# Seven block products in eleven groups instead of seven, with the corner sums taken in mid-group

## The chip, the cores and the metric

The kernel runs on one core of one Trainium2 chip. The metric is the device time of one execution in microseconds (us). TensorE (PE) multiplies matrices into PSUM, which has eight banks here: four for accumulators (`acc_ps`), four for small results (`sm_ps`). VectorE (DVE) and ScalarE (ACT) do elementwise work, GpSimd (POOL) a little of it, and SyncE (SP) starts the loads. Each engine runs its own instructions strictly in the order in which the program has them, and waits where an operand or a buffer isn't ready.

## The reference

A trunk of two layers over 256 tokens of width 2048: an mLSTM mixer, a gated ConvFFN, a differential attention, a second ConvFFN, all in float32. What touches the change:

```python
def mlstm_mixer(xn, w_in, b_igate, b_fgate, w_hnorm, w_out):
    proj = xn @ w_in
    q, k, v, o, ig, fg = jnp.split(proj, M_SPLITS, axis=-1)
    ...
    h = rms_norm(h.transpose(0, 2, 1, 3), w_hnorm).astype(xn.dtype)
    h = h.reshape(B, S, M_HV) * jax.nn.sigmoid(o)
    return h @ w_out

def shared_kv(h, g_kv, w_kv, pos):
    kv = rms_norm(h, g_kv) @ w_kv
    k, v = jnp.split(kv, (A_HQK,), axis=-1)
    ...

def diff_attention(xn, k, v, pos, w_q, lam_q1, lam_k1, lam_q2, lam_k2, g_subln, w_o, lambda_init):
    ...
    lam = (jnp.exp(jnp.sum(lam_q1 * lam_k1)) - jnp.exp(jnp.sum(lam_q2 * lam_k2)) + lambda_init)
    ...
        pd = p[:, :, 0] - lam * p[:, :, 1]
        outs.append(jnp.einsum('bhqk,bkhv->bqhv', pd.astype(vb.dtype), vb))
    ...
    return o.reshape(B, S, A_HV) @ w_o
```

Heads are 256 wide in V; `o` is the output gate. Each of the four projections that the change speaks of (gate `o`, `w_out`, attention's V, `w_o`) is a product of 256 x 2048 by 2048 x 2048.

## The kernel before, in words

**Products in split form.** TensorE multiplies float32 operands in a reduced form, so each operand is split in a high and a low part: ACT copies the high part of a weight tile (`w2`, L376), DVE subtracts it from the tile for the low part (L377). A product is three matmuls: high by high, low by high, high by low.

**Groups.** A projection by tokens (`gemm_tokens`, L437) runs over four groups of 512 columns. A group takes 16 k-tiles of 128 rows; two accumulators `a` and `b` of 128x512, one for each half of the tokens, collect it. Four k-tiles come with one load of 1 MB (`raw`, four buffers), and are split in two granules of two k-tiles, each into one `w2` buffer. There are five `w2` buffers (`HL`), so a split waits until the granule five earlier has been multiplied. A dense granule is 12 matmuls of 128x512.

**Sevenths.** `gemm_sevenths` does four of the 16 k-tiles of a group, the quad, by Winograd's form of the 2x2 block product: for each pair of k-tiles seven block products of 128x256 instead of eight, times three, 42 matmuls in all (L493) instead of 24 of 128x512. It needs differences of the weights (`diff`, DVE, L449 to L451), splits of the three blocks and the four differences (L458, L459), and mixed forms of the other operand (`mix`: four sums on DVE, L531 to L534, a split on ACT and DVE, L536 and L537). Two more accumulators `c` and `d` (named `mix`) collect what belongs to more than one corner. They are buffers of `sm_ps`. At the group's end the corners are summed. In the gate projection `mixed_up` does it: a copy on ACT (L559), four sums of 128x256 on DVE (L560 to L563), two of 128x512 into a and b (L564, L565). In the output projections `mixed_in` sums straight into the residual stream, a copy and seven instructions (L572 to L579).

**Where.** `OUT_AT = (8, 10)` sets the k-tiles of the pairs, that is the third load of a group. Sevenths are used in the gate projection for groups 1 and 2, in `m_w_out` for groups 1 to 3, in `w_o` for groups 2 and 3. Gate groups 0 and 3, `m_w_out` group 0, `w_o` groups 0 and 1 and all of attention's V are dense. The FFN's down projections have sevenths of their own, with other k-tiles. The mixed forms of the norm's output (`x_mixed`) are made at once ahead of the gate projection by `mix_again`; those of the heads' outputs come with the head whose tiles they are, `mix_scaled` in `turned` and `placed`.

**What sets the order.** `tick()` counts granules, and `later(n, fn)` emits a step n granules on: head steps, parameters, lambda (`lambda_col`, a small matmul into `lam_ps`, L916, nine granules after the parameters' loads). The order of each engine is then fixed at build by a scheduler from priorities (program order) and readiness, so a later step can stand ahead of an earlier one. `evac_o` (gate), `evac_v` and `residual` empty the accumulators at a group's end: in the gate projection tanh on ACT (L804) and a product on DVE (L805), then transposes on TensorE (`hn_ps`, L357), split into `mo` (L306, L307), which are the operands of `m_w_out`.

Of the kernel before, what the change touches and what calls it, by code (L numbers as in the profile page):

```python
# [10 lines left out]
F32 = mybir.dt.float32  # L11
# [27 lines left out]
RAW = 4  # L39
OUT_AT = (8, 10)  # L40
MIXED = (4, 12, 20)
# [27 lines left out]
def trunk(  # L69
# [25 lines left out]
    def small_ps(name):  # L95
        return sm_ps.tile([P, 512], F32, tag="sm", name=name)
# [366 lines left out]

    def gemm_sevenths(xs, mixed, w, col0, groups, evac, at):


        kn, raws = len(xs), {}
        for g in groups:
# [3 lines left out]
            while k0 < kn:  # L472
                if k0 in at:
                    if c is None:
                        c, d = small_ps("mix"), small_ps("mix")
                    parts = sevenths(w, col0 + g * G, k0, min(2, (kn - k0) // 2))
                    for p, (b1, b2, b3, t1, t3, t2, t4) in enumerate(parts):
# [16 lines left out]
                        if p < len(parts) - 1:  # L494
                            tick()
                    k0 += 4
                else:
# [7 lines left out]
                tick()  # L505
            evac(g, (a, b), (c, d))

# [45 lines left out]

    def mixed_up(ps, mix):

        (a, b), (c, d) = ps, mix
        u = tmp("mx")
        x, y = block(F32, "mixed_a"), block(F32, "mixed_b")
        act.activation(x[1], c[:, :T], AF.Copy)  # L559
        dve.tensor_tensor(u, c[:, T:], x[1], op=ALU.add)  # L560
        dve.tensor_tensor(y[1], d[:, T:], u, op=ALU.add)
        dve.tensor_tensor(x[0], d[:, :T], u, op=ALU.add)
        dve.tensor_tensor(y[0], d[:, :T], y[1], op=ALU.add)  # L563
        dve.tensor_tensor(a, a, x[2], op=ALU.add)  # L564
        dve.tensor_tensor(b, b, y[2], op=ALU.add)  # L565

# [97 lines left out]
    def mlstm(norm):  # L664
# [85 lines left out]

        def evac_v(g, ps):
            for c in range(2):
                h = 2 * g + c
                v[h] = [scaled_split(ps[t][:, c * VD:(c + 1) * VD], norm.rt[:, t:t + 1], f"mv{h}_{t}", T + 2) for t in range(2)]
                for vh, vl, _ in v[h]:
                    pool.memset(vh[:, T:].bitcast(F32), 1.0)
                    pool.memset(vl[:, T:].bitcast(F32), 0.0)
                later(1 + 4 * c, lambda h=h: weights(h))
# [37 lines left out]

        def evac_o(g, ps, mix=None):
            if mix is not None:
                mixed_up(ps, mix)
            for c in range(2):  # L800
# [26 lines left out]
        later_parameters_in()  # L827
        x_mixed = {k: mix_again(xs[k], xs[k + 1]) for k in OUT_AT}
        gemm_tokens(xs, w, 2 * HQK + HV, [0], evac_o)
        gemm_sevenths(xs, x_mixed, w, 2 * HQK + HV, [1, 2], evac_o, OUT_AT[:1])  # L830
        gemm_tokens(xs, w, 2 * HQK + HV, [3], evac_o)
        return outs, outs_mixed

# [90 lines left out]
    def attention(norm):  # L924
# [54 lines left out]

        def evac_v(g, ps):  # L980
            for c in range(2):
# [30 lines left out]
        gemm(norm.sets[1], w_kv, 0, range(8), rotated(k, "ak", softmax))  # L1012
        gemm_tokens(norm.sets[1], w_kv, AQK, range(4), evac_v)
        return outs, outs_mixed
# [3 lines left out]
    def later_parameters_in():  # L1018

        with tc.issue_after(loads[-1].ins):  # L1020
# [5 lines left out]
            later_layers.append(rotary_tables())  # L1026
        later(9, lambda: later_layers.append(lambda_col()))

# [9 lines left out]
    norm_f0 = Norm([(gains, G_F0)], "f0")  # L1038
    gemm_tokens(outs, m_w_out[0], 0, [0], residual(norm_f0))
    gemm_sevenths(outs, outs_mixed, m_w_out[0], 0, range(1, NG - 1), residual(norm_f0), OUT_AT[:1])  # L1040
    gemm_sevenths(outs, outs_mixed, m_w_out[0], 0, [NG - 1], residual(norm_f0), OUT_AT[:1])

# [4 lines left out]
    gemm_tokens(outs, w_o[0], 0, range(2), residual(norm_f1), lead=2)  # L1047
    gemm_sevenths(outs, outs_mixed, w_o[0], 0, range(2, NG), residual(norm_f1), OUT_AT[:1])

# [91 lines left out]
```

## Time and profile before

| what | us |
|---|---|
| median of 3 runs (2253.45 to 2253.83) | 2253.77 |
| the profiled execution | 2253.21 |
| its span | 2251.4 |
| TensorE busy | 2239.6 |
| DVE busy | 1789.7 |
| ACT busy | 1292.0 |

The profiled execution is 1.8 us longer than its span, which is what lies around the first and last instruction. A busy TensorE is a chain of pipelined matmuls; its share of the span says how little it waits. A row of the view of groups ends with busy time, mean ns of one, and idle time before it with the releasers. In a timeline the first two figures are start and duration in us, and the bracket names what an engine waited for.

By the timeline, the stages that matter lie at: gate projection 233 to 305, `m_w_out` 305 to 396, attention's V 1318 to 1420, `w_o` 1420 to 1515.

### The profile page before, as it was taken

To read this page: it belongs to the slowest core of one execution; us is meant where nothing else is said; L and a number is where in the kernel's file an instruction comes from. 1 tells how busy PE (TensorE), PEld (TensorE's weight loads), DVE (VectorE), ACT (ScalarE), POOL (GpSimd) and SP (SyncE) were. 2 spreads that over 40 slices of the span, in tenths; PEclk is the share of its full clock that TensorE was granted. 3 is DMA by queue.
4 is the path that set the end of the run, shared out by engine and by line. 5 is a ranking of instruction groups with operands and counts; after the bars stand their busy time and mean duration, and the time that the engine had idled before them with its cause. 6 is when DMAs were issued, how large, how long until landed. Compare 5 with 4: busy or idle time off the path is not lost.

```text
span 2251.4 us, 33430 instructions
## 1 busy us (share of the span) xinstructions
PE 2239.6 (99%) x12843; PEld 1954.1 (87%) x12843; DVE 1789.7 (79%) x2964; ACT 1292.0 (57%) x1994; POOL 125.0 (6%) x305
## 2 busy tenths in 40 slices
PE   9999999999999999999999999999999999999998
PEld 9888888888888888888888888888888888888888
DVE  5756778887888877879998885677877988778896
ACT  5456655655555555656654556566555555556554
POOL 0014200000000000000022103200000000000000
PEclk9999999999999999999999999999999999999999
DMA  7554546555555755545566555465555457555464
GB/s 265 188 169 157 166 171 205 192 191 187 187 170 179 242 187 187 187 150 203 189 208 194 163 167 169 150 206 187 187 187 187 156 191 239 191 189 191 146 215 150
DMA packets 325348, 419.04 MB, mean 186 GB/s; under 512 B 9070, under 2 KB 238788, under 8 KB 325188
## 3 DMA queue, kind: packets, MB, share of 16 engines
q1 hardware_dynamic: 325156, 416.89, 56.4%
q8 instruction: 101, 1.65, 0.3%
q14 instruction: 59, 0.48, 0.1%
q10 hardware_dynamic: 32, 0.01, 0.0%
HBM read 414.77 MB, written 2.10 MB: 185 GB/s over the span
## 4 chain that ended last, share of the span: by engine, by line
PE 97%; DVE 1%; POOL 1%; issue 1%; ACT 0%; DMA 0%; DVEq 0%; SPq 0%; POOLq 0%
PE acc L411 54%; PE acc L503 16%; PE acc L437 12%; PE mix L493 6%; PE acc L493 4%; PE acc L634 2%; PE acc L521 1%; PE val_ps L335 1%; PE turn_ps L231 1%; PE as_ps L955 0%; DVE w L377 0%; POOL rs_u L279 0%; POOL rs_u L280 0%; DMA pos_i<-in_positions_dram 0%; POOL rs_u L281 0%
## 5 line engine op out<-in xcount | busy, mean ns | idle before, releaser
L377 DVE TENSOR_TENSOR w<-raw,w 128x1024 fp32r<-128x1024 f32 x679 | 825.9, 1220 | 280.1 <-ACT w L376 277.5
L376 ACT ACTIVATE w<-raw 128x1024 fp32r<-128x1024 f32 x679 | 713.9, 1058 | 491.7 <-PE acc L411 324.8
L411 PE MATMUL acc<-x_f,w 128*128 128x512 f32 (+1 forms) x5632 | 988.1, 337 | 0.0
L411 PEld LDWEIGHTS acc<-x_f,w 128*128 128x128 f32 x5632 | 861.7, 188 | 123.2
L503 PE MATMUL acc<-w,hid 128*128 128x512 f32 x1080 | 268.2, 394 | 0.0
L503 PEld LDWEIGHTS acc<-w,hid 128*128 128x128 f32 x1080 | 195.4, 188 | 39.0
L411 PE MATMUL acc<-x_at,w 128*128 128x512 f32 (+1 forms) x1024 | 182.1, 338 | 0.0
L411 PEld LDWEIGHTS acc<-x_at,w 128*128 128x128 f32 x1024 | 156.8, 188 | 22.2 <-issue 0.3
L458 ACT ACTIVATE w<-diff 128x1024 fp32r<-128x1024 f32 x89 | 94.1, 1057 | 111.1 <-DVE diff L451 81.7
L417 ACT ACTIVATE low<-acc 128x256 f32<-128x256 f32 x216 | 79.3, 386 | 135.4 <-PE acc L411 132.6
L459 DVE TENSOR_TENSOR w<-diff,w 128x1024 fp32r<-128x1024 f32 x89 | 108.7, 1221 | 40.9 <-ACT w L458 40.3
L437 PE MATMUL acc<-w,x_a 128*128 128x512 f32 x576 | 138.0, 396 | 0.0
L437 PEld LDWEIGHTS acc<-w,x_a 128*128 128x128 f32 x576 | 106.8, 188 | 24.2
L493 PE MATMUL mix<-w,mix 128*128 128x256 f32 x801 | 119.3, 281 | 0.0
L418 DVE TENSOR_TENSOR acc<-acc,low 128x256 f32<-128x256 f32 x216 | 84.5, 430 | 37.7 <-ACT low L417 37.3
L493 PEld LDWEIGHTS mix<-w,mix 128*128 128x128 f32 x801 | 107.0, 188 | 2.4 <-DVE w L459 0.2
L848 ACT ACTIVATE c<-u,conv 128x256 f32<-128x256 f32 x176 | 98.2, 593 | 5.5 <-DVE u L846 5.2
L939 POOL TENSOR_TENSOR sw<-sw,sin_t 32x256 f32<-32x256 f32 x32 | 42.0, 1328 | 1033.8 <-DVE sw L938 1022.5
L458 ACT ACTIVATE w<-raw 128x768 fp32r<-128x768 f32 x89 | 74.7, 840 | 37.9 <-PE acc L503 27.4
L437 PE MATMUL acc<-w,x_at 128*128 128x512 f32 x384 | 91.8, 396 | 0.0
L459 DVE TENSOR_TENSOR w<-raw,w 128x768 fp32r<-128x768 f32 x89 | 84.6, 951 | 2.8 <-ACT w L458 2.7
L493 PE MATMUL acc<-w,hid 128*128 128x256 f32 x450 | 86.3, 281 | 0.0
(302 smaller groups left out, 2320.4 us busy)
## 6 DMA issues: line engine op xcount, KB each, us to landing
raw<-in_w_up_dram SPq DMA_DIRECT2D x176, 1024.0 KB
raw<-in_w_down_dram SPq DMA_DIRECT2D x79, 1024.0 KB
raw<-in_m_w_in_dram SPq DMA_DIRECT2D x46, 1024.0 KB
raw<-in_w_kv_dram SPq DMA_DIRECT2D x32, 1024.0 KB
raw<-in_m_w_out_dram SPq DMA_DIRECT2D x16, 1024.0 KB
raw<-in_w_q_dram SPq DMA_DIRECT2D x16, 1024.0 KB
raw<-in_w_o_dram SPq DMA_DIRECT2D x16, 1024.0 KB
raw<-in_w_down_dram SPq DMA_DIRECT2D x15, 512.0 KB
```

The lines of the kernel that those rows point to most:

```text
L376: act.activation(w2[:, :hc, 0], part, AF.Copy)
L377: dve.tensor_tensor(w2[:, :hc, 1], part, w2[:, :hc, 0].bitcast(F32), op=ALU.subtract)
L411: pe.matmul(to, a, b, start=(k == 0 and o == 0), stop=(k == kn - 1 and o == len(ops) - 1))
L417: act.activation(low, p[:, T:], AF.Copy)
L418: dve.tensor_tensor(p[:, :T], p[:, :T], low, op=ALU.add)
L437: pe.matmul(ps[t], a[:, s], b, start=(k == 0 and o == 0), stop=(k == kn - 1 and o == 2))
L458: act.activation(w2[:, :m, 0], src, AF.Copy)
L459: dve.tensor_tensor(w2[:, :m, 1], src, w2[:, :m, 0].bitcast(F32), op=ALU.subtract)
L493: pe.matmul(to, u, v, start=start and o == 0, stop=end and o == 2 and to is not a and to is not b, skip_group_check=True)
L503: pe.matmul(ps, u[:, s], v, start=(k0 + i == 0 and o == 0), stop=(k0 + i == kn - 1 and o == 2), skip_group_check=True)
L634: pe.matmul(ps[j], a, b, start=(k == 0 and o == 0 and j % 2 == 0), stop=(k == KD - 1 and o == 2), skip_group_check=True)
L848: act.activation(c, u, AF.Identity, bias=cw[:, 3, f:f + 1], scale=cw[:, 2, f:f + 1])
```

## The change

- `OUT_AT` becomes (4, 6): the quad is a group's second load, and the heads whose outputs get mixed forms are 2 and 3 instead of 4 and 5.
- `gemm_sevenths` takes `mid`. With it, c and d are buffers of `acc_ps`, and `mid` is emitted right behind the quad's last granule; the evacuation gets what it returns. `mixed_up` is cut in two: `mixed_sums` (copy and four sums) for mid-group, `mixed_up` (two sums into a and b) for the end. For the output projections `mid` is `mixed_in`.
- The mixed forms of the norm's output are made by `forms_of`, two and four granules into the projection's first group, for the gate and for attention's V.
- Sevenths in attention's V for groups 1 to 3, and in `m_w_out` for group 0 too: 11 groups (gate 2, `m_w_out` 4, V 3, `w_o` 2) instead of 7 (2, 3, 0, 2).
- Lambda comes 40 granules after the parameters instead of 9.

```diff
-OUT_AT = (8, 10)
+OUT_AT = (4, 6)
...
-    def gemm_sevenths(xs, mixed, w, col0, groups, evac, at):
+    def gemm_sevenths(xs, mixed, w, col0, groups, evac, at, mid=None):
...
                     if c is None:
-                        c, d = small_ps("mix"), small_ps("mix")
+                        if mid is None:
+                            c, d = small_ps("mix"), small_ps("mix")
+                        else:
+                            c, d = (acc_ps.tile([P, 2 * T], F32, tag="acc", name="mix") for _ in range(2))
...
+                    if mid is not None and k0 == at[-1]:
+                        sums = mid(g, (c, d))
                     k0 += 4
...
-            evac(g, (a, b), (c, d))
+            evac(g, (a, b), (c, d) if mid is None else sums)
...
-    def mixed_up(ps, mix):
-
-        (a, b), (c, d) = ps, mix
+    def forms_of(xs, forms):
+        for n, k in enumerate(OUT_AT):
+            later(2 + 2 * n, lambda k=k: forms.update({k: mix_again(xs[k], xs[k + 1])}))
+
+    def mixed_sums(g, mix):
+
+        c, d = mix
...
         dve.tensor_tensor(y[0], d[:, :T], y[1], op=ALU.add)
-        dve.tensor_tensor(a, a, x[2], op=ALU.add)
-        dve.tensor_tensor(b, b, y[2], op=ALU.add)
+        return x[2], y[2]
+
+    def mixed_up(ps, sums):
+        for p, x in zip(ps, sums or ()):
+            dve.tensor_tensor(p, p, x, op=ALU.add)
...
-        def evac_v(g, ps):
+        def evac_v(g, ps, sums=None):
+            mixed_up(ps, sums)
...
-        x_mixed = {k: mix_again(xs[k], xs[k + 1]) for k in OUT_AT}
-        gemm_tokens(xs, w, 2 * HQK + HV, [0], evac_o)
-        gemm_sevenths(xs, x_mixed, w, 2 * HQK + HV, [1, 2], evac_o, OUT_AT[:1])
-        gemm_tokens(xs, w, 2 * HQK + HV, [3], evac_o)
+        col, x_mixed = 2 * HQK + HV, {}
+        forms_of(xs, x_mixed)
+        gemm_tokens(xs, w, col, [0], evac_o)
+        gemm_sevenths(xs, x_mixed, w, col, [1, 2], evac_o, OUT_AT[:1], mixed_sums)
+        gemm_tokens(xs, w, col, [3], evac_o)
...
-        gemm_tokens(norm.sets[1], w_kv, AQK, range(4), evac_v)
+        xs, x_mixed = norm.sets[1], {}
+        forms_of(xs, x_mixed)
+        gemm_tokens(xs, w_kv, AQK, [0], evac_v)
+        gemm_sevenths(xs, x_mixed, w_kv, AQK, range(1, 4), evac_v, OUT_AT[:1], mixed_sums)
...
-        later(9, lambda: later_layers.append(lambda_col()))
+        later(40, lambda: later_layers.append(lambda_col()))
...
-    gemm_tokens(outs, m_w_out[0], 0, [0], residual(norm_f0))
-    gemm_sevenths(outs, outs_mixed, m_w_out[0], 0, range(1, NG - 1), residual(norm_f0), OUT_AT[:1])
-    gemm_sevenths(outs, outs_mixed, m_w_out[0], 0, [NG - 1], residual(norm_f0), OUT_AT[:1])
+    gemm_sevenths(outs, outs_mixed, m_w_out[0], 0, range(NG), residual(norm_f0), OUT_AT[:1], mixed_in)
...
-    gemm_sevenths(outs, outs_mixed, w_o[0], 0, range(2, NG), residual(norm_f1), OUT_AT[:1])
+    gemm_sevenths(outs, outs_mixed, w_o[0], 0, range(2, NG), residual(norm_f1), OUT_AT[:1], mixed_in)
```

Three places show how the order moves. The line numbers of the changed kernel are its own: L509 is a dense matmul of `gemm_sevenths`, L497 a block product, L569 the copy and L570 to L573 the sums of `mixed_sums`, L578 `mixed_up`, L817 the gate's tanh. The bracket at a row's end names the engines or load queues (DMAHW) that the instruction waits for.

First TensorE at the end of gate group 1. Before, group 1's products into d (`mix_2658`) stand last, and group 2 opens a and b (`acc_2773`, `acc_2774`) at once:

```order
L493 MATMUL mix_2658<-w2_2674,mix_2283 128x256
L493 MATMUL mix_2658<-w2_2674,mix_2284 128x256
L493 MATMUL mix_2658<-w2_2674,mix_2283 128x256 x2
L493 MATMUL mix_2658<-w2_2674,mix_2284 128x256
L493 MATMUL mix_2658<-w2_2674,mix_2283 128x256
L503 MATMUL acc_2773<-w2_2777,x_a_0_172 128x512 [waits Activation_49]
L503 MATMUL acc_2773<-w2_2777,x_a_0_172 128x512
L503 MATMUL acc_2774<-w2_2777,x_a_0_172 128x512 x2
```

Now dense granules stand last, and group 2's a (`acc_2763`) runs ahead of its b, with a wait for DVE at its first matmul:

```order
L509 MATMUL acc_2581<-w2_2734,x_a_15_635 128x512 x3
L509 MATMUL acc_2582<-w2_2734,x_a_15_635 128x512 x3
L509 MATMUL acc_2763<-w2_2767,x_a_0_172 128x512 [waits DVE_49]
L509 MATMUL acc_2763<-w2_2767,x_a_0_172 128x512 x2
L509 MATMUL acc_2763<-w2_2767,x_a_1_175 128x512 x3
L509 MATMUL acc_2763<-w2_2830,x_a_2_244 128x512 x3
L509 MATMUL acc_2763<-w2_2830,x_a_3_247 128x512 x3
L497 MATMUL acc_2763<-w2_2853,x_a_5_291 128x256 x3
```

In the built program `acc_2763` has the bank of `mix_2615`, group 1's c, and the wait is for L570, its last reader.

Second ACT at the same place. Before, the copy of c stands ahead of the splits of group 2's quad:

```order
L376 ACTIVATE w2_2846<-raw_2829 128x2x512 [waits PE_49]
L306 ACTIVATE mo3_2578<-hn_ps_2570,half_h_145 128x256 [waits DVE_49]
L559 ACTIVATE mixed_a_2752<-mix_2657 128x256
L458 ACTIVATE w2_2869<-raw_2863 128x3x256 [waits DMAHW6_49,PE_49,Activation_49]
L458 ACTIVATE w2_2872<-diff_2865 128x4x256 [waits DVE_49,PE_49,Activation_49]
```

Now it stands behind the third of these splits, whose buffer held `w2_2734`:

```order
L458 ACTIVATE w2_2856<-diff_2849 128x4x256 [waits DVE_49,Activation_49]
L306 ACTIVATE mo1_2567<-hn_ps_2559,half_h_145 128x256 [waits DVE_49]
L306 ACTIVATE mo2_2575<-hn_ps_2570,half_h_145 128x256 [waits PE_49]
L458 ACTIVATE w2_2859<-raw_2847 128x3x256 [waits PE_49,Activation_49]
L306 ACTIVATE mo3_2578<-hn_ps_2570,half_h_145 128x256 [waits DVE_49]
L569 ACTIVATE mixed_a_2678<-mix_2615 128x256
```

The copy has moved from ahead of a split for the next group to behind one that waits for TensorE.

Third DVE at the end of gate group 2. Before, the first sum (L560) stands behind head 3's last `mo` and ahead of group 3's next split:

```order
L377 TENSOR_TENSOR w2_3061<-raw_3059,w2_3061 128x2x512 [waits DMAHW1_49,DVE_49,Activation_49]
L377 TENSOR_TENSOR w2_3076<-raw_3059,w2_3076 128x2x512 [waits DVE_49,Activation_49]
L307 SCALAR_TENSOR_TENSOR mo7_2811<-hn_ps_2803,half_h_145,mo7_2811 128x256 [waits Activation_49]
L560 TENSOR_TENSOR mx_2955<-mix_2861,mixed_a_2956 128x256 [waits Activation_49]
L377 TENSOR_TENSOR w2_3093<-raw_3091,w2_3093 128x2x512 [waits DMAHW2_49,DVE_49,Activation_49]
```

Now a split that group 3 needs (`w2_3083`, in the buffer of group 2's last weights) and head 3's mixed forms (`sum_2821`, `mix_2827`) stand ahead of it:

```order
L307 SCALAR_TENSOR_TENSOR mo7_2814<-hn_ps_2806,half_h_145,mo7_2814 128x256 [waits Activation_49]
L377 TENSOR_TENSOR w2_3083<-raw_3081,w2_3083 128x2x512 [waits DMAHW2_49,Activation_49]
L539 TENSOR_TENSOR sum_2821<-mx_2817 128x128 [waits Activation_49]
L537 TENSOR_TENSOR sum_2821<-mx_2817,mx_2818 128x128 [waits Activation_49]
L538 TENSOR_TENSOR sum_2821<-sum_2821,mx_2817 128x128 [waits DVE_49]
L540 TENSOR_TENSOR sum_2821<-mx_2818,sum_2821 128x128 [waits DVE_49]
L543 TENSOR_TENSOR mix_2827<-sum_2821,mix_2826 128x512 [waits Activation_49]
L570 TENSOR_TENSOR mx_2907<-mix_2845,mixed_a_2908 128x256 [waits Activation_49]
```

Group 3's first matmul waits for this L570 in the same way: its a has the bank of `mix_2845`, group 2's c.

More of the change, by code (lines that the diff above doesn't have):

```diff
@@ L795, in scaled, with evac_o @@
             hn[h] = normed_rows(banks, y, block(F32, f"hn{h}")[:2])
-        def evac_o(g, ps, mix=None):
-            if mix is not None:
-                mixed_up(ps, mix)
+        def evac_o(g, ps, sums=None):
+            mixed_up(ps, sums)
             for c in range(2):
@@ L978, in turned, with evac_v @@
             pt[h] = split_weights(t_ps, h, "pt")
-        def evac_v(g, ps):
+        def evac_v(g, ps, sums=None):
+            mixed_up(ps, sums)
             for c in range(2):
```

## The prediction

> **What bounds the kernel now.** I read the page first: span, busy shares, clock, chain.
>
> ```profile
> span 2251.4 us, 33430 instructions
> PE 2239.6 (99%) x12843; PEld 1954.1 (87%) x12843; DVE 1789.7 (79%) x2964; ACT 1292.0 (57%) x1994; POOL 125.0 (6%) x305
> ...
> PEclk9999999999999999999999999999999999999999
> ...
> PE 97%; DVE 1%; POOL 1%; issue 1%; ACT 0%; DMA 0%; DVEq 0%; SPq 0%; POOLq 0%
> ```
>
> TensorE is busy 99% of the span at full granted clock, and 97% of the chain that ended last is its own work. So the second view is what TensorE waits for, summed over the span: the waits from the profile's own list.
>
> ```profile
> PE warm_ps L130 <- DVE warm L126: 1.0, 1, 1.0
> PE acc L634 <- ACT w L626: 0.8, 1, 0.8
> PE lam_ps L916 <- ACT hn L348: 0.7, 1, 0.7
> PE acc L634 <- DVE w L627: 0.5, 2, 0.3
> PE hn_ps L357 <- DVE conv L1034: 0.3, 1, 0.3
> ```
>
> That is 3.3 us in five places; none is longer than 1.0 us, and after the first matmuls of the kernel only the 0.7 and the 0.3 are left. The time is therefore matmul work plus waits of TensorE plus the two ends. A change pays by every matmul it takes out, and costs by every new wait of TensorE. Nothing else counts, unless DVE (79%) or ACT get so late that TensorE waits for them.
>
> **Term 1, the products: −2.48 us.** The chain of waits gives the cadence of both forms.
>
> ```profile
> 644.53 5.58 PE acc L503 x24
> 650.10 0.34 PE mix L493 x3
> ...
> 655.06 0.93 PE acc L503 x4
> ```
>
> Four dense k-tiles are 24 matmuls of 128x512 in 5.58 us. The same four k-tiles by seven block products are 42 matmuls of 128x256 (eight pieces of 3, 6, 9, 3, 3, 6, 9 and 3), from 650.10 to 655.06, 4.96 us. Each further group by sevenths saves 0.62 us. There are four: three in the attention's V projection, one in the m_w_out projection. 4 x 0.62 = 2.48.
>
> **Term 2, waits that go: −1.04 us.** The two waits in TensorE's timeline of before:
>
> ```profile
> 248.82 0.66 PE L357 MATMUL hn_ps<-ident,o 128*128 128x128 f32 x4 [0.29 <-DVE conv L1034]
> ...
> 253.45 0.38 PE L916 MATMUL lam_ps<-pr,ones 128*128 128x2 f32 x2 [0.75 <-ACT hn L348]
> ```
>
> The 0.75 is lambda's matmul, which stands in gate group 1 in the order of before and needs one of the four sm_ps buffers. The change moves it into m_w_out group 0, among dense matmuls. The 0.29 is a transpose that waits for another of these buffers; c and d of the gate groups no longer take two of the four. I count both as gone; if both stay, +1.04.
>
> **Term 3, place A (gate group 1 to 2): +2.8 us.** Before, group 1's c and d lie in sm_ps, and group 2's a and b only need banks that were free long ago. Round the end of group 1 the timeline of before shows:
>
> ```profile
> 257.69 12.50 PE L503 MATMUL acc<-w,x_a 128*128 128x512 f32 x53
> ...
> 259.93 0.38 ACT L559 ACTIVATE mixed_a<-mix 128x256 f32<-128x256 f32 x1
> 260.73 0.85 ACT L458 ACTIVATE w<-raw 128x768 fp32r<-128x768 f32 x1 [0.43 <-ACT mixed_a L559]
> ...
> 263.44 0.48 DVE L307 SCALAR_TENSOR_TENSOR mo<-hn_ps,half_h,mo 128x256 fp32r<-128x256 f32 x1
> 263.84 0.41 DVE L560 TENSOR_TENSOR mx<-mix,mixed_a 128x256 f32<-128x256 f32 x1
> ```
>
> The sum mx comes at 263.84, some 4 us after the copy, and TensorE goes on through 53 matmuls without a gap. After the change c and d lie in acc_ps, whose four banks are a, b, c, d of one group. Group 2's a takes the bank of group 1's c, and its first matmul waits for mx. The code asks for the sums right behind the quad, but in the order of the changed kernel they are late: the copy stands on ACT behind the split w2_2859. That split's buffer is the fifth of five and held the last weights of group 1, so it waits for group 1's last matmul. From there the chain runs over these durations:
>
> ```profile
> L458 ACT ACTIVATE w<-raw 128x768 fp32r<-128x768 f32 x89 | 74.7, 840 | 37.9 <-PE acc L503 27.4 <-PE acc L493 5.3 <-ACT c L848 3.0
> L459 DVE TENSOR_TENSOR w<-raw,w 128x768 fp32r<-128x768 f32 x89 | 84.6, 951 | 2.8 <-ACT w L458 2.7
> L307 DVE SCALAR_TENSOR_TENSOR mo<-hn_ps,half_h,mo 128x256 fp32r<-128x256 f32 x16 | 7.5, 479 | 7.0 <-ACT mo L306 7.0
> ```
>
> 0.84 (ACT's split) + 0.95 (DVE's) + 0.48 (mo3) + 0.41 (mx) = 2.68; ACT's mo3 and copy run beside DVE's split. Two neighbours on an engine overlap by some 0.09 (263.84 − 263.44 for the 0.48 before it), a hand-over costs about 0.04: 2.6. DVE had work of some 4 us ahead of mx at this point before, part of which may stand ahead of the split again, so I take 2.8 and a range of 2.6 to 4. The second sum that b needs ends 1.0 us after mx (3 x 0.33); 12 matmuls of a (2.8 us) hide it.
>
> **Term 4, place B (gate group 2 to 3): +5.1 us.** Group 3 is dense, its first matmul needs the bank of group 2's c. Here ACT's copy stands behind the split w2_3083, which waits for group 2's last matmul, and behind head 3's mixed forms.
>
> ```profile
> L376 ACT ACTIVATE w<-raw 128x1024 fp32r<-128x1024 f32 x678 | 713.4, 1059 | 491.7 <-PE acc L411 324.8 <-PE acc L437 66.6 <-PE acc L503 45.3
> L377 DVE TENSOR_TENSOR w<-raw,w 128x1024 fp32r<-128x1024 f32 x678 | 825.2, 1221 | 280.1 <-ACT w L376 277.5
> L536 ACT ACTIVATE mix<-sum 128x512 fp32r<-128x512 f32 x26 | 16.0, 617 | 1.0 <-DVE sum L534 1.0
> L537 DVE TENSOR_TENSOR mix<-sum,mix 128x512 fp32r<-128x512 f32 x26 | 17.8, 684 | 0.0
> ...
> 299.49 0.28 DVE L533 TENSOR_TENSOR sum<-mx 128x128 f32<-128x128 f32 x1
> ...
> 300.33 0.29 DVE L534 TENSOR_TENSOR sum<-mx,sum 128x128 f32<-128x128 f32 x1
> ```
>
> 1.06 + 1.22 + 1.13 (four sums, 299.49 to 300.62) + 0.62 + 0.68 + 0.41 = 5.12, the same chain of ACT and DVE in turn; overlaps of 0.09 and hand-overs of 0.04 nearly cancel. Range 4.7 to 5.3. b needs its sum 1.0 us later, behind 21 matmuls.
>
> **Term 5, attention: +1.0 us.** DVE is what could be short here. Windows of before, over the start of the V projection:
>
> ```profile
> 1318.50:1344.00 25.50, 25.50 (x122) 21.01 (x121) 20.94 (x49) 13.31 (x30) 1.60 (x2) 1.00 0.52 165
> 1344.00:1369.50 25.50, 25.50 (x124) 21.09 (x123) 14.21 (x22) 14.07 (x27) 4.78 (x16) 1.00 0.54 168
> ...
> L459 DVE TENSOR_TENSOR w<-diff,w 128x1024 fp32r<-128x1024 f32 x89 | 108.7, 1221 | 40.9 <-ACT w L458 40.3
> L449 DVE TENSOR_TENSOR diff<-raw 128x1024 f32<-128x1024 f32 x37 | 45.1, 1219 | 4.2 <-DMA raw<-in_w_down_dram 3.3 <-DMA raw<-in_w_o_dram 0.8
> L450 DVE TENSOR_TENSOR diff<-raw,diff 128x512 f32<-128x512 f32 x37 | 25.3, 684 | 0.1
> L451 DVE TENSOR_TENSOR diff<-raw,diff 128x512 f32<-128x512 f32 x37 | 25.3, 684 | 0.2
> ```
>
> DVE (fourth figure) is busy 20.94 of 25.5 us, then 14.21. The change adds two mixed forms (each two adds of 0.41, four sums 1.13, one 0.68: 2.6; both 5.3) in group 0, and per group by sevenths 1.22 + 2 x 0.68 + 2 x (0.95 + 1.22) = 6.9 for 2.4 of dense splits, plus sums of 1.6 and 1.4. Per 25.5 us that is 20.94 + 5.3 = 26.2 at the worst, then 14.21 + 7.5 = 21.7. Group 0 is short by 0.7 if all falls into that window; some can lie in the next: 0 to 1.2, I take 0.5. At the end of V, place C, w_o's first matmul waits for the sum behind split, form and copy again, but the split there waits for a granule one earlier: 1.06 + 1.22 + 0.68 + 0.41 = 3.4 against 2.8 of TensorE's work (12 x 0.233): 0.3 to 1.5, I take 0.5.
>
> **At nothing.** In m_w_out and w_o the sums (mixed_in) stand in the order well ahead of the next group's first matmul, 8 k-tiles of work behind the quad (11 us) hide them. If that cover fails, the price is that of A, 2.7 us, for each group. Loads per group stay the same in the gate groups; in V each quad adds a diff tile to the four raw buffers, with DMA at 0.52 to 0.54 of its time. Matmuls of the forms: none.
>
> **A colder clock, if TensorE idles.** No wait of before is over 1.0 us, so no row shows what the array does after 5 us of idling. The start shows how a cold array runs:
>
> ```profile
> 1.04 3.17 PE L130 MATMUL warm_ps<-warm 128*128 128x128 bf16 x28 [1.04 <-DVE warm L126]
> ...
> 4.86 1.50 PE L130 MATMUL warm_ps<-warm 128*128 128x128 bf16 x24
> ```
>
> 113 ns each at first, 62 ns 0.7 us later: half speed for about 3.2 us, which is 28 x 51 ns = 1.4 us lost. The Trainium skill, "TensorE: Matmul & The Clock Gate", section "What's actually happening", states the rule: the gate halves the clock after an idle window of about 3.4 us, which runs free of the program, and gives it back after one busy window. By that rule A (2.8 us) costs nothing more; in B's 5.1 us a whole window lies with a chance of (5.1 − 3.4) / 3.4, one half, an estimate from that page.
>
> **The sum.** −2.48 − 1.04 + 2.8 + 5.1 + 1.0 = +5.4. Against the profiled execution's 2253.21 (span 2251.4 and 1.8 around it) that gives 2258.6; the median of the three runs, 2253.77, lies 0.56 above it, and a forecast of a median is 2253.77 + 5.4 = 2259.2.
>
> **The rivals.** No change or faster (chance 0.17 that neither wait is felt): the mechanism is the order on ACT. If the copies of A and B ran when their quad is done, some 10 us ahead, the two waits would vanish; then 2259.2 − 7.9 = 2251.3 is left, 2250.3 if attention costs nothing. For it: the code asks for the sums there. Against it: engines run in their order, and in both places a split that waits for TensorE's last matmul stands ahead. It decides from the point where that split gets its buffer 2.7 us earlier. Only one of the two is felt (0.15): 2259.2 less 2.8 or 5.1, 2256.4 or 2254.1. The colder clock (0.20): +1.4 at B, 2260.6, or at A too, 2262. For it: the start's 113 ns; against it: nothing of before idles that long. DVE as the bound in V (0.05): 7.5 us a group too much for its slack at the wrong moments, +2 to +4, 2261 to 2263. The forecast itself: 0.43, from 2257.8 to 2260.7 by its bounds.
>
> **How the numbers follow.** 0.2% (4.5 us) is about what a measurement of this kernel can tell from no change: the bounds are 2249.3 and 2258.3. Slower: the clock, DVE, and three quarters of the forecast, 0.57. Faster: 0.05, for a wait removed that I don't see, since even the first rival ends at 2250.3. Same: the rest, 0.38. The range from 2250.0 to 2262.0 takes in both kinds of the first rival and one or two cold stretches, and leaves out the worst of DVE and sums of several bad ends.
>
> **What would show it.** Right: TensorE's waits list two new rows, acc <- DVE mx (or mixed), one near 2.8 and one near 5.1 us, at the starts of gate groups 2 and 3, and the rows of lam_ps and hn_ps gone; ACT's copy mixed_a behind the 128x768 and the 128x1024 splits; 128x256 matmuls four groups more. Wrong: gaps under 1 us there; 128x512 matmuls 470 ns apart instead of 233 for 3 us behind a gap (the clock); gaps in the V projection of over 1.5 us in sum.

## The result and the profile after

The changed kernel takes 2269.03 us (median of 6 runs, 2268.19 to 2269.89), the kernel before, on the same chip, 2253.78 (6 runs, 2253.45 to 2253.86). The ratio is 1.0068, 95% interval 1.0055 to 1.0080: slower by 15.25 us, where +5.4 was predicted. The profiled execution took 2268.26, its span 2266.2.

The page of after, with the rows that answer to those of before:

```profile
span 2266.2 us, 33655 instructions
PE 2244.0 (99%) x12915; PEld 1959.5 (86%) x12915; DVE 1819.3 (80%) x3022; ACT 1296.9 (57%) x2008; POOL 137.9 (6%) x305
...
PE 92%; DVE 3%; issue 2%; POOL 1%; ACT 1%; DMA 0%; DVEq 0%; SPq 0%; ACTq 0%; POOLq 0%
```

TensorE still fills 99% of the span, but of the chain that ended last its own work is now 92% for 97%: elsewhere the end was set by others. The waits of TensorE in after (engine, line, operand, releaser: us in all, times, longest):

```profile
PE acc L437 <- DVE mx L570: 6.4, 2, 5.2
PE acc L509 <- DVE mx L570: 4.2, 1, 4.2
...
PE an_ps L357 <- ACT nrm L348: 0.5, 1, 0.5
PE acc L497 <- DVE mix L543: 0.3, 1, 0.3
...
PE acc L509 <- ACT w L376: 0.2, 1, 0.2
```

The rows of `lam_ps` and `hn_ps` are gone. In their place stand the foreseen two, 4.2 us (place A) and 5.2 us (place B), and 1.1 us at `w_o`'s first matmul (place C, the rest of the 6.4).

How the clock stood at the two places, in windows of after (stretch and its us, then busy time of PE, PEld, DVE, ACT and POOL; the third figure from the end is the granted clock):

```profile
258.20:262.44 4.24, 0.07 (x1) 0.00 (x0) 3.62 (x7) 2.76 (x6) 0.00 (x0) 0.98 0.58 220
262.44:265.20 2.76, 2.76 (x7) 2.18 (x8) 2.65 (x6) 0.93 (x3) 0.00 (x0) 0.50 0.85 245
...
292.00:294.50 2.50, 2.50 (x6) 2.02 (x7) 2.50 (x6) 0.71 (x2) 0.00 (x0) 0.50 0.02 7
294.50:297.00 2.50, 2.50 (x8) 1.93 (x8) 1.25 (x4) 0.96 (x3) 0.00 (x0) 0.63 0.00 0
297.00:300.50 3.50, 3.50 (x18) 2.79 (x17) 0.00 (x0) 0.00 (x0) 0.00 (x0) 1.00 0.00 0
```

Behind both waits TensorE runs at half clock: 7 matmuls in 2.76 us, 6 in 2.50. The clock records in the trace put the halved stretches at 3.41 us from 262.24 and 6.83 us, twice as long, from 289.55. Of these TensorE worked in some 3.2 us (262.44 to 265.65) and 4.4 us (291.96 to 296.37), at half speed, so 1.6 + 2.2 = 3.8 us were lost on top of the waits. The Trainium skill, "TensorE: Matmul & The Clock Gate", section "What's actually happening", has the gate halve the clock after an idle window of about 3.4 us and give it back after a busy one. This trace agrees in the length, for both stretches are whole numbers of 3.41 us. But the window ahead of the second halving (286.13 to 289.55) wasn't idle throughout: TensorE worked in 0.59 us of it.

Where the 15 us lie is read from the first and last starts of dense matmuls, line by line. Before:

```profile
L503 PE MATMUL acc<-w,hid x1080: 387/394/407, 644.4 to 2209.3; 128*128 128x512 f32 x180
L503 PE MATMUL acc<-w,mo x216: 387/395/487, 328.6 to 396.1; 128*128 128x512 f32 x108
L503 PE MATMUL acc<-w,x_a x144: 388/394/481, 233.2 to 281.9; 128*128 128x512 f32 x144
L503 PE MATMUL acc<-w,ao x144: 387/394/486, 1469.4 to 1514.7; 128*128 128x512 f32 x144
...
L437 PE MATMUL acc<-w,x_at x384: 387/394/482, 1318.5 to 1420.1; 128*128 128x512 f32 x192
L437 PE MATMUL acc<-w,ao x192: 387/394/483, 1420.4 to 1469.1; 128*128 128x512 f32 x192
...
L437 PE MATMUL acc<-w,mo x96: 387/394/479, 305.4 to 328.3; 128*128 128x512 f32 x96
```

After:

```profile
L509 PE MATMUL acc<-w,hid x1080: 387/394/404, 655.3 to 2224.1; 128*128 128x512 f32 x180
L509 PE MATMUL acc<-w,mo x288: 387/394/482, 317.3 to 407.5; 128*128 128x512 f32 x144
...
L509 PE MATMUL acc<-w,x_a x144: 387/395/793, 233.6 to 286.3; 128*128 128x512 f32 x144
L509 PE MATMUL acc<-w,ao x144: 388/394/481, 1481.0 to 1526.4; 128*128 128x512 f32 x144
...
L437 PE MATMUL acc<-w,ao x192: 387/394/499, 1431.2 to 1480.6; 128*128 128x512 f32 x192
...
L437 PE MATMUL acc<-w,x_at x96: 387/394/480, 1328.2 to 1354.0; 128*128 128x512 f32 x96
```

Differences of these starts give the stages (the last column holds the prediction's terms, spread over them):

| stage | before, us | after, us | change | forecast |
|---|---|---|---|---|
| up to the gate's `x_a` L503/L509 | 233.2 | 233.6 | +0.4 | 0 |
| gate, to the first matmul with `mo` | 72.2 | 83.7 | +11.5 | +6.9 (2.8 + 5.1 − 1.04) |
| `m_w_out`, to its last dense matmul | 90.7 | 90.2 | −0.5 | −0.6 |
| to V's first matmul (first FFN and more) | 922.4 | 920.7 | −1.7 | 0 |
| V, to `w_o`'s first matmul | 101.9 | 103.0 | +1.1 | −0.9 (1.0 − 1.86) |
| `w_o`, to its last dense matmul | 94.3 | 95.2 | +0.9 | 0 |
| second FFN, to the last with `hid` | 694.6 | 697.7 | +3.1 | 0 |
| from there to the end of the span | 42.1 | 42.1 | 0 | 0 |

In sum +14.8, the difference of the spans.

The stages don't hold quite the same work. Nine products of attention (`val_ps`, 128x256) and four transposes (`an_ps`) that ran in V's stage before run in `w_o`'s now, and two matmuls of the second FFN (0.5 us) that ran ahead of `w_o`'s last one run behind it. The first move is worth 1.5 us (see the kernel with V dense, below). With this put right V lost 2.6 us, `w_o` nothing, and the second FFN 2.6.

### The profile page after: what moved, and what is told of

The parts are those of the page before. It is cut to its first block, busy times and chain, and to the rows that moved or that the text cites. A ratio compares the mean times of both kernels' runs of the same rounds, so it can differ in the third digit from the quotient of the medians.

```text
span 2266.2 us, 33655 instructions
## 1 busy us (share of the span) xinstructions
PE 2244.0 (99%) x12915; PEld 1959.5 (86%) x12915; DVE 1819.3 (80%) x3022; ACT 1296.9 (57%) x2008; POOL 137.9 (6%) x305
## 4 chain that ended last, share of the span: by engine, by line
PE 92%; DVE 3%; issue 2%; POOL 1%; ACT 1%; DMA 0%; DVEq 0%; SPq 0%; ACTq 0%; POOLq 0%
PE acc L411 53%; PE acc L509 16%; PE acc L437 8%; PE mix L497 5%; PE acc L497 4%; PE acc L647 2%; DVE w L377 1%; PE acc L527 1%; PE turn_ps L231 1%; DVE w L459 1%; PE val_ps L335 1%; ACT w L376 0%; POOL rs_u L279 0%; POOL rs_u L281 0%; PE as_ps L969 0%
## 5 line engine op out<-in xcount | busy, mean ns | idle before, releaser
L377 DVE TENSOR_TENSOR w<-raw,w 128x1024 fp32r<-128x1024 f32 x671 | 815.3, 1221 | 254.5 <-ACT w L376 252.0
L376 ACT ACTIVATE w<-raw 128x1024 fp32r<-128x1024 f32 x671 | 703.4, 1058 | 479.2 <-PE acc L411 325.1
L509 PE MATMUL acc<-w,hid 128*128 128x512 f32 x1080 | 268.0, 394 | 0.0
L509 PEld LDWEIGHTS acc<-w,hid 128*128 128x128 f32 x1080 | 195.4, 188 | 38.8
L458 ACT ACTIVATE w<-diff 128x1024 fp32r<-128x1024 f32 x97 | 102.6, 1057 | 123.3 <-DVE diff L451 87.4
L459 DVE TENSOR_TENSOR w<-diff,w 128x1024 fp32r<-128x1024 f32 x97 | 118.6, 1223 | 52.8 <-ACT w L458 52.3
L497 PE MATMUL mix<-w,mix 128*128 128x256 f32 x873 | 130.2, 282 | 0.2 <-ACT w L458 0.2
L497 PEld LDWEIGHTS mix<-w,mix 128*128 128x128 f32 x873 | 116.2, 188 | 2.8 <-ACT w L458 0.4
L418 DVE TENSOR_TENSOR acc<-acc,low 128x256 f32<-128x256 f32 x216 | 84.6, 430 | 39.9 <-ACT low L417 39.8
L953 POOL TENSOR_TENSOR sw<-sw,sin_t 32x256 f32<-32x256 f32 x32 | 46.7, 1476 | 1047.6 <-DVE sw L952 1042.1
L458 ACT ACTIVATE w<-raw 128x768 fp32r<-128x768 f32 x97 | 81.5, 840 | 47.0 <-PE acc L509 22.8
L459 DVE TENSOR_TENSOR w<-raw,w 128x768 fp32r<-128x768 f32 x97 | 92.5, 953 | 6.5 <-ACT w L458 6.4
L497 PE MATMUL acc<-w,hid 128*128 128x256 f32 x450 | 86.4, 281 | 0.0
L864 DVE SCALAR_TENSOR_TENSOR c<-u,conv,c 128x254 f32<-128x254 f32 x176 | 78.9, 480 | 1.3
```

Of the source, the lines that this page charges most:

```text
L376: act.activation(w2[:, :hc, 0], part, AF.Copy)
L377: dve.tensor_tensor(w2[:, :hc, 1], part, w2[:, :hc, 0].bitcast(F32), op=ALU.subtract)
L418: dve.tensor_tensor(p[:, :T], p[:, :T], low, op=ALU.add)
L458: act.activation(w2[:, :m, 0], src, AF.Copy)
L459: dve.tensor_tensor(w2[:, :m, 1], src, w2[:, :m, 0].bitcast(F32), op=ALU.subtract)
L497: pe.matmul(to, u, v, start=start and o == 0, stop=end and o == 2 and to is not a and to is not b, skip_group_check=True)
```

## Experiments

Each kernel was timed in five rounds beside the kernel before, whose median was 2253.69, 2253.64 and 2253.61 for the first four, the next four and the last four. Edits are against the changed kernel unless said otherwise.

**The sums' buffers taken early.** The builds tell why the sums came late: the pool of activation blocks gives its buffers in the order of the program, and the copy's target `mixed_a` had to wait for a turn behind `mo` (A) or behind head 3's mixed forms (B). A one-element write by GpSimd to each of the three buffers of the sums, emitted a group ahead, takes that turn early; nothing else changes.

```diff
+    def hold():
+        held.append((tmp("mx"), block(F32, "mixed_a"), block(F32, "mixed_b")))
+        for part in (held[-1][0], held[-1][1][2], held[-1][2][2]):
+            pool.memset(part[:, :1], 0.0)
...
-        u = tmp("mx")
-        x, y = block(F32, "mixed_a"), block(F32, "mixed_b")
+        u, x, y = held.pop(0)
```

`hold()` is called ahead of gate group 0 and behind group 1's quad. ACT's order then has the copy right behind the quad:

```order
L376 ACTIVATE w2_2743<-raw_2726 128x2x512 [waits PE_49]
L579 ACTIVATE mixed_a_2262<-mix_2621 128x256 [waits PE_49]
L376 ACTIVATE w2_2776<-raw_2774 128x2x512 [waits DMAHW4_49,PE_49]
L348 ACTIVATE hn7_2562<-val_ps_2464,yh_2490 128x256 [waits DVE_49,Pool_49]
```

> The changed kernel, but in the gate projection the three buffers of the sums (mx, mixed_a, mixed_b) are taken early: GpSimd writes one element of each before group 0's heads (for group 2: right behind group 1's sums) take theirs. In the order, ACT's copy then stands right behind the quad, ahead of mo0 to mo3 and ahead of head 3's mixed forms. Theory (the sums are late by their place in the order, because a pool hands out its buffers in the order of first use, and the shared bank turns that lateness into a wait of TensorE, behind which the clock is halved): the waits of 4.2 and 5.2 us at gate groups 2 and 3 go, and with them both stretches at half clock, 1.6 and 2.2 us: 13.2 us less, 2269.0 to about 2255.8. Rival (VectorE is full in the gate projection, 24 of 26 us before, and the extra work has to come out somewhere): TensorE then waits for a split of the weights or for a transpose instead, and less than 7 us are won, 2262 or more.

Measured: 2254.46 us (2253.80 to 2254.89), ratio 1.0004 (0.9995 to 1.0013), 14.6 below the changed kernel. In the waits of this run nothing is left at A and B; the longest behind the start is C:

```profile
PE acc L437 <- DVE mx L580: 1.2, 1, 1.2
```

Its windows round the two places, with the clock at full:

```profile
255.00:265.00 10.00, 10.00 (x55) 8.51 (x54) 9.10 (x17) 6.83 (x13) 0.00 (x0) 1.00 0.70 234
285.00:297.00 12.00, 12.00 (x58) 9.74 (x56) 10.08 (x18) 7.34 (x12) 0.00 (x0) 1.00 0.26 88
```

The gate takes 70.4 us (232.9 to 303.3), 13.3 less than in after, which is 4.2 + 5.2 + 3.8 = 13.2. Against before it is 1.8 shorter, of which the two vanished waits are 1.04. So the place of one copy in the order carried nearly all of the loss. The rest of the change, four groups more by sevenths, gains nothing that can be measured.

**c and d in banks of their own.** The rival lever: keep the sums in mid-group, but c and d in `sm_ps`, so that the next group doesn't need their banks.

```diff
-                            c, d = (acc_ps.tile([P, 2 * T], F32, tag="acc", name="mix") for _ in range(2))
+                            c, d = small_ps("mix"), small_ps("mix")
```

> The changed kernel, with c and d in the four small buffers as before the change, but the sums still asked for in mid-group. The sums stay as late in the order as in the changed kernel. Theory (the shared bank makes the wait): no first matmul of a group waits for mx any more, at gate groups 2 and 3 nor at the start of w_o; 4.2 + 5.2 + 1.1 us and the 3.8 us of half clock go, and up to 1 us of waits for small buffers comes back: 2255 to 2256. Rival (VectorE or ACT are too late anyway, whichever bank it is): TensorE waits for weights or transposes in these places instead, over 2262.

Measured: 2266.26 us (2264.01 to 2267.81), 1.0058 (1.0045 to 1.0072). A miss. The gate was cured (its `m_w_out` starts at 305.3, as before), and no matmul waits for `mx` any more, so the shared bank made these waits. But round the end of V other waits came, and `w_o` took 104.2 us (1420.3 to 1524.5) for 95.2:

```profile
PE an_ps L357 <- ACT nrm L348: 6.0, 3, 3.8
PE acc L506 <- ACT w L376: 3.1, 2, 1.9
```

Behind the longest of them, 3.8 us, the clock was halved too, for 3.41 us from 1437.5. In V, c and d now take two of the four small banks, which the attention's products (`val_ps`) and transposes (`an_ps`) need as well. The profile names the transposes' operand (`nrm`, from ACT) as what came last, and not a bank. That the lack of banks made it late is argued, not shown.

**The clock kept up.** 60 and 80 matmuls of 128x128 in bf16 on a constant tile, held in their place on TensorE, fill the waits at A and B. They compute nothing that is used.

```diff
             evac(g, (a, b), (c, d) if mid is None else sums)
+            if busy and g in busy:
+                busy_pe(busy[g])
...
+        gemm_sevenths(xs, x_mixed, w, col, [1, 2], evac_o, OUT_AT[:1], mixed_sums, {1: 60, 2: 80})
```

> The changed kernel, with small bfloat16 matmuls into a buffer nobody reads between gate groups 1 and 2 (60 of 62 ns, 3.7 us) and between groups 2 and 3 (80, 5.0 us), in TensorE's order directly ahead of the waiting matmul. The output is not touched. The waits for mx stay as they are in length (4.2 and 5.2 us from the end of the group before), but the array isn't idle in them. Theory (half clock costs 1.6 + 2.2 us behind the idle stretches): granted clock 1.0 throughout, matmuls of 128x512 233 ns apart right behind the waits, 2269.0 to about 2265.2. Rival (the slow matmuls behind the waits are not the idle clock but contention or the memory of the other engines catching up): they stay slow, no change, 2269.

Measured: 2264.31 us (2263.85 to 2264.68), 1.0047 (1.0034 to 1.0059), 4.7 below the changed kernel. The timeline at A, and the windows behind both places:

```profile
257.69 3.52 PE L145 MATMUL busy_ps<-warm 128*128 128x128 bf16 x60
262.02 3.05 PE L528 MATMUL acc<-w,x_a 128*128 128x512 f32 x12 [0.81 <-DVE mx L591]
```

```profile
262.00:265.00 3.00, 2.98 (x13) 2.45 (x14) 2.82 (x7) 1.15 (x3) 0.00 (x0) 1.00 0.87 266
290.00:294.00 4.00, 3.93 (x17) 3.22 (x18) 3.79 (x10) 1.68 (x4) 0.00 (x0) 1.00 0.00 0
```

The sums come as late as ever, yet TensorE now does 13 matmuls in 3 us where it did 7. `m_w_out` starts 3.9 us earlier (313.4 for 317.3); 0.4 of this lies ahead of the gate (233.2 for 233.6), so 3.5 us are won in it, against 3.8 worked out for the clock. The rival, that the matmuls are slow for another reason, is out. So the price of the half clock is shown by itself.

**V dense again.** All four groups of V by plain products.

```diff
-        forms_of(xs, x_mixed)
-        gemm_tokens(xs, w_kv, AQK, [0], evac_v)
-        gemm_sevenths(xs, x_mixed, w_kv, AQK, range(1, 4), evac_v, OUT_AT[:1], mixed_sums)
+        gemm_tokens(xs, w_kv, AQK, range(4), evac_v)
```

> The changed kernel, with attention's V projection dense in all four groups as before the change. The three sevenths groups there save 1.86 us of matmuls, and the trace after has waits of 0.5, 0.3, 0.2 and 1.1 us there, 2.1 in sum. Theory (V by sevenths gains nothing, since new waits give its saving back): 2269.0 + 1.9 - 2.1, no change within 1 us, about 2268.8, and the wait for mx at the start of w_o gone. Rival (V by sevenths is worth its 1.9 us, and what V lost is something else): 2270.9.

Measured: 2265.49 us (2264.52 to 2266.92), 1.0053 (1.0040 to 1.0065). Both numbers were missed: it is 3.5 below the changed kernel. V takes 100.4 us (1328.1 to 1428.5) for 103.0: in this program sevenths in V cost 2.6 instead of saving 1.86. The remaining 0.9 is mostly the second FFN, 696.6 us (1524.0 to 2220.6) for 697.7, though it is no part of the edit and has a new wait of 1.0 us for a split. That was the first sign of the finding on its matmuls below.

V before the change was dense too, and took 101.9 us. The 1.5 us between it and this run are the products and transposes that moved on to `w_o`'s stage, which takes 95.6 us here for 94.3.

**Buffers early in V too.** The same `hold()` for V's groups, on top of the gate's.

> The run with buffers held early in the gate projection (2254.46), with the same done in attention's V projection: the three buffers of the sums are taken before group 0's evacuation, and right behind the sums of the group before. Theory (the sums of V are late by their place in the order too): the wait of 1.2 us for mx at w_o's first matmul goes; the smaller waits in V (for a mixed form, for a weight split, for a transpose, together some 2 us of gaps) stay, being of another kind: 2254.5 less 1.3, about 2253.2. Rival (VectorE is short in V, whatever the order): the wait for mx turns into another, no change, 2254.5.

Measured: 2256.13 us (2255.84 to 2256.70), 1.0012 (1.0003 to 1.0021). The wait at C is gone, and another stands in V:

```profile
PE acc L511 <- ACT w L376: 1.3, 1, 1.3
```

V takes 102.4 us (1315.8 to 1418.2), 0.3 less than with the gate's `hold()` alone. The sums weren't what limits V; the splits take their place. The second FFN took 698.0 us (1513.8 to 2211.8) for 695.9, and that made the kernel slower than the first experiment's.

**Gate buffers early, V dense.**

> Buffers held early in the gate projection, and attention's V dense. The sevenths then left beyond those before the change are the one in m_w_out (0.62 us). With V dense the changed kernel ran 3.5 us faster. Theory (V by sevenths costs 3.3 us of gaps for 1.9 us of matmuls, and the rest by cadence): 2254.5 less 1.4 to 3.5, 2251.0 to 2253.1, which is at best 0.1% faster than before. Rival (the 3.5 us were the FFN's cadence, not V): 2254.5.

Measured: 2253.88 us (2253.67 to 2254.40), 1.0002 (0.9993 to 1.0011). `w_o`'s last dense matmul came at 1512.0, 2.7 us ahead of before, and the second FFN lost it again: 697.9 us (to 2209.9) for 694.6. In it are the two matmuls that moved (0.5 us) and one new wait of 0.6 us for a split (`mix` L497, 2200.0); the rest, some 2 us, is in no wait.

**What slows the second FFN.** From the 167th of its some 4050 matmuls on, its order is the same in before and after. What differs is where the pools put the operands. Two kernels test this: 64 bytes of a constant tile at the start of SBUF, which shifts all that follows alike, and 64 bytes between the pool of activation blocks and that of weights, which shifts one against the other.

```diff
+    gap = ctx.enter_context(tc.tile_pool(name="gap", bufs=1))
+    pad = gap.tile([P, 16], F32, name="pad")
+    pool.memset(pad, 0.0)
```

> The changed kernel with 64 more bytes per partition at the start of SBUF, written once and never read: every operand's address moves by 64 bytes, the order of every engine stays word for word. In the second FFN the changed kernel's 128x512 matmuls are 232.55 ns apart, before 231.46, and every run whose operands lay at the changed kernel's addresses showed 232.5 to 232.6 there, every other 231.3 to 232.1. Theory (the addresses of the operands set the cadence by up to 0.5%): if it is the address itself, the cadence in the second FFN changes by 0.3 ns or more, a time 1 us or more off 2269. Rival (it is the order of the program or the clock): the cadence stays 232.5 to 232.6.

> The changed kernel with the 64 bytes put between the buffers of the activations and those of the weights: only the weights' addresses and those of the small work buffers move by 64 bytes, relative to the activations. Order unchanged. Theory (what matters is where weights and activations lie towards one another, or the weights' address): the cadence in the second FFN moves by 0.3 ns or more from 232.55. Rival (order or clock): 232.5 to 232.6, about 2269.

Measured: 2268.70 us (2267.83 to 2269.20) with all shifted, the changed kernel's time; 2270.05 (2269.23 to 2271.34) with the weights shifted. In the latter the second FFN got shorter (1531.4 to 2227.1, 695.7 us for 697.7), the stages up to `w_o` longer:

```profile
L512 PE MATMUL acc<-w,hid x1080: 387/394/404, 658.4 to 2227.1; 128*128 128x512 f32 x180
...
L512 PE MATMUL acc<-w,ao x144: 387/394/483, 1485.8 to 1531.4; 128*128 128x512 f32 x144
```

The pitch of a matmul is the time from its start to the next start. The mean pitch of the 128x512 matmuls over the whole second FFN, without gaps over 40 ns above the usual 232, fell from 232.5 to 231.8 ns; with all shifted alike it stayed at 232.5. (Taken so it is 231.7 in the kernel before, where the expectation gives 231.46.) So the pitch depends on the place of weights and activations relative to each other.

The longer stages with the weights shifted are the first FFN with what follows it (923.1 us for 920.7) and the gate (85.7 us for 83.7). In the gate the waits are those of the changed kernel, 4.2 and 5.2 us, but the half clock behind A lasted 6.83 us instead of 3.41. So it did with all shifted alike, where the gate took 85.1 us.

**The same gap in the kernel before.** The cross-check: an edit of before that changes no computation and no order around the stages.

> The kernel before with 64 bytes between the buffers of the activations and those of the weights; nothing else, and no change of order. Theory (where weights and activations lie towards one another sets the cadence of TensorE, in the kernel before as well): the cadence of the 128x512 matmuls in the two FFNs moves by 0.3 ns or more in at least one of them from 232.7 and 231.5, and the time by 1 to 3 us from 2253.7 with no wait changed. Rival: same cadence, 2253.7.

Measured: 2255.38 us (2254.82 to 2255.51), 1.0007 (0.9999 to 1.0016), +1.8. The waits are those of before, and the second FFN, 1513.6 to 2211.4, takes 697.8 us for 694.6:

```profile
L506 PE MATMUL acc<-w,hid x1080: 387/394/404, 644.1 to 2211.4; 128*128 128x512 f32 x180
...
L506 PE MATMUL acc<-w,ao x144: 387/394/486, 1468.2 to 1513.6; 128*128 128x512 f32 x144
```

The first FFN with what follows it (396.6 to 1317.3) takes 920.7 us for 922.4. So 64 bytes alone, with the matmuls of both stages in the order of before, make −1.7 and +3.2 us, as large as the −1.7 and +3.1 that after has there. Here both come from the pitch; the mean for 128x512 in the second FFN is 232.7 ns for 231.7.

**The gate's part alone.** Before, with the gate's quad in the second load and its sums in mid-group, and nothing else; the heads' mixed forms stay with heads 4 and 5.

> The kernel before, with the gate projection's part of the change alone: quad in the second load there, c and d in the accumulators' banks, sums asked for in mid-group. Attention, both output projections and lambda are as before. Heads 2 and 3 have no mixed forms here. Theory (the gate part alone makes the loss): TensorE waits for mx at group 2's first matmul some 4.2 us as in the changed kernel, and at group 3's less, by the forms that no longer stand ahead (1.13 + 0.62 + 0.68 = 2.4), about 2.8; half clock 1.6 us behind the first wait, 0 to 1.7 behind the second: 2253.7 + 8.6 to 10.3, 2262.3 to 2264, give or take 2 for the cadence of the FFNs. Rival (the loss came from several parts together): under 2258.

Measured: 2256.91 us (2256.01 to 2257.45), 1.0014 (1.0006 to 1.0023); the rival's figure. Of the two waits only A is there:

```profile
PE acc L509 <- DVE mx L570: 4.0, 1, 4.0
```

with the half clock behind it, in a window of this run:

```profile
262.00:265.50 3.50, 3.29 (x8) 2.61 (x9) 3.29 (x9) 1.46 (x4) 0.00 (x0) 0.50 0.81 262
```

The gate takes 77.3 us (233.3 to 310.6), +5.1. The theory had left 2.8 us at B, by taking the forms' own 2.4 us off the 5.2. Without them the copy runs at 278.6 already and the sum at 280.8, 6.5 us ahead of group 3's first matmul. So B isn't a property of the sums in mid-group: it needs head 3's mixed forms ahead of them, which came from moving `OUT_AT` (lambda's place is the only other difference in the gate). And the half clock lasted 6.83 us here behind a wait of 4.0, against 3.41 behind 4.2 in after.

**A faster version.** Gate buffers early and V dense, with a gap of 64 or 32 bytes (`[P, 16]` or `[P, 8]`) between the two pools.

> The version with gate buffers held early and V dense (2253.88; its first FFN's cadence was 232.9 and 117.6, its second's 232.3 and 118.4), with 64 bytes between activations and weights. Up to the second FFN it was 2.7 us ahead of the kernel before, and lost 3.2 there by its cadence. Theory (placement): another cadence in the second FFN; with the kernel before's it would be 2250.7, with the worst seen (233.2) 2255.5. Rival: unchanged, 2253.9.

> The same with 32 bytes instead of 64. Theory (placement, and a step of 32 bytes is enough): again another cadence, between 2250.7 and 2255.5. Rival (only steps of 64 bytes count): as without, 2253.9.

Measured: 2252.32 us (2251.83 to 2252.57), 0.9994 (0.9985 to 1.0003), and 2250.65 (2250.22 to 2251.56), 0.9988 (0.9979 to 0.9997). The second is the fastest of all, 3.0 us (0.13%) below before, at the lower edge of what its expectation gave, and some of that is placement found by trial. Its longest wait behind the start is one of 0.7 us:

```profile
PE mix L500 <- ACT w L461: 0.7, 1, 0.7
```

## Why the prediction was wrong

Its direction was right and its mechanism too: the two waits stand where they were put. The size was wrong by 9.4 us in the spans (+14.8 for +5.4), and the time fell outside the range. Three steps failed: the half clock was kept out of the sum (3.8 us), V was sized at 1.0 us of waits (4.5), and place A at 2.8 (4.2). By its steps:

- **Terms 1 and 2.** `m_w_out` gained 0.5 for 0.62. The waits for `lam_ps` and `hn_ps` are gone, the gate by itself is 1.8 shorter (first experiment) where 1.04 was counted; lambda's two matmuls left it too, for `m_w_out`. In V the saved 1.86 didn't arrive, see term 5.
- **Term 3, place A: 4.2 for 2.8.** The step that failed is the value taken near the low end of a range of 2.6 to 4; the wait lies above its upper end. The chain of waits of after shows what stood in it:

```profile
257.70 1.07 ACT w L458
...
258.79 1.23 DVE w L459
260.01 0.79 DVE mo L307 x2
260.80 0.87 DVE w L459
261.66 0.40 DVE mo L307
262.06 0.34 DVE mx L570
...
262.44 0.79 PE acc L509
```

The predicted steps are the last ones (0.87, 0.40, 0.34). Ahead of them DVE had the split before that one (1.23), begun only when ACT's half of it was done at 258.76, and two `mo` (0.79). I had summed the chain from ACT's split on, as if DVE were free when ACT is done. The prediction named the "some 4 us" of DVE's work and then took a value near the other end; DVE's backlog was the bound.

- **Term 4, place B: 5.2 for 5.1.** The chain has the forecast steps in their order:

```profile
286.81 1.06 ACT w L376
...
287.90 1.22 DVE w L377
289.12 0.20 DVE sum L539
289.33 0.21 DVE sum L537
...
290.21 0.64 ACT mix L542
...
290.88 0.69 DVE mix L543
291.57 0.34 DVE mx L570
```

- **The colder clock, a rival at 0.20, came true** at both places: 3.8 us for the 1.4 or 2.8 allowed. The price of one cold stretch was read from the start, 28 matmuls; behind B it was two windows of 3.41 us long. What failed is that only a wait holding a whole idle window was counted, which left A out, although its range went up to 4, and gave B one half. The window ahead of B's halving had 0.59 us of work in it.
- **Term 5, V and place C: 4.5 for 1.0.** Against dense V in the same program V lost 2.6 where −0.86 was forecast, so its costs were 2.6 + 1.86 = 4.5. The 0.7 that DVE was to be short of in group 0 didn't show: no wait lies there. C was 1.1 us for 0.5, and three more waits are listed in V's groups by sevenths (0.5, 0.3, 0.2), 2.1 us in sum. The list counts a wait only from the modelled end of the matmul before (394 ns after its start for 128x512, where the next usually starts after 232) and leaves the shortest out. Counted from start to start, V's matmuls come 4.3 us later than at their usual 232 and 118 ns in after, in 18 places, and 0.3 us in dense V. Their usual pitch is the same, 232.5 ns in both. So the loss is waits, most of them short, and not pitch. The rival of DVE as the bound, at 0.05, is right in size (+2 to +4): DVE works 84.6 of V's 103.0 us in after, 65.0 of 100.4 with V dense. Which engine would have to be faster was not told apart.
- **At nothing.** The prediction took stages without a changed instruction as unchanged. The first FFN and what follows it took 1.7 us less, the second FFN 3.1 more. Of this 3.1 some 2.1 is pitch, 0.5 the two matmuls that moved, 0.5 short waits. The gap between pools makes shifts of that size in before. So about 2 us each way is put down to placement, and the two nearly cancel. `w_o`'s +0.9 is work that came from V's stage.

In one line: 9.4 over = 1.4 (A) + 0.1 (B) + 3.8 (clock) + 3.5 (V) − 0.1 (`w_o`) + 2.6 − 1.7 (FFNs) + 0.4 and 0.1 (ahead of the gate, `m_w_out`) − 0.7 (the gate's other work). Here V, `w_o` and the second FFN are put right for the work that moved between them.

The first rival, that neither wait is felt, put 2251.3; the kernel with the buffers taken early is that case, and gave 2254.46. Its gate gained as that rival says, V (+2.3 against dense V) and the second FFN (+1.3) took it back.

## What to carry to other kernels

Where a sum frees the bank that the next group opens, look up in the built order what stands ahead of it on its engine, and which buffer put it there: a pool that hands out buffers in program order can hold an urgent copy behind work that has nothing to do with it, and a tiny early write to the target mended that for 14.6 us here. Price a wait of TensorE of 4 us or more with the half clock behind it, 1.4 to 3.0 us each time in these runs. Before two kernels are compared stage by stage, count what ran in each stage: the scheduler moves work across the boundaries. Before a gain or loss of a few us in 2250 is put down to an edit, read the stages that the edit didn't touch.

## What the runs showed of the hardware

- **The clock halves in whole windows, and a window needn't be idle.** In each run the changes of the granted clock lie whole multiples of 3.41 us apart, so the run can be cut into windows of that length. Every window ahead of a halving held at most 1.20 us of TensorE's work (in after 0.00 and 0.59, in the gate's part alone 0.91); no window with 1.84 us or more was followed by one (TensorE's work as the profile models it). The clock came back behind windows with 2.75 us of work or more, and not behind those with 2.64 or less. Between these bounds the runs show nothing. So a wait of 4.2 us cost one halved window in after and two in both kernels shifted by 64 bytes, depending on where it fell. As an estimate from 3.41 and 1.20, a wait of 4.4 us can't miss, for it leaves one window with 1.2 us of work or less. No wait between 1.9 us (not followed by a halving) and 3.8 us occurred.
- **Small matmuls keep it up.** With 60 and 80 of them in the waits, and gaps of 0.81 and 0.75 us left, the clock stayed at 1.00.
- **Matmul pitch depends on placement.** The mean pitch of the 128x512 matmuls in the second FFN ran from 231.4 to 233.0 ns over these kernels, 0.7%, with the clock at 1.00 and longer gaps left out. A gap of 64 bytes between the pools of activations and weights moved it from 232.5 to 231.8 in the changed kernel and from 231.7 to 232.7 in before; a shift of both alike left it at 232.5. Why isn't known from these runs.
